# Down projection of a streaming-encoder layer: six of eleven channel pairs through seven block products, the rest plain, and the residual parked in DRAM

## The chip, the cores and the metric

The kernel runs on one core of a Trainium2 chip. A core has a matrix engine (TensorE, PE in the profile; its weight loads are PEld), a vector engine (VectorE, DVE), a scalar engine (ScalarE, ACT), GpSimd (POOL) and SyncE (SP), which here issues nearly all DMAs. Each runs its own instruction list in order; semaphores join them. The metric is the time of one execution on the device in microseconds (us); lower is better.

## The reference, cut to what matters

One layer: three token mixers, a cross-attention into a memory, and a gated MLP, all in float32, on 512 tokens of 1024 channels. The change is in the last step of the MLP:

```python
def conv_ffn(h, w_up, conv_w, conv_b, w_down):
    u = causal_dwconv(h @ w_up, conv_w) + conv_b      # 1024 -> 2 x 2816, then 3 taps over time
    a, b = jnp.split(u, 2, axis=-1)
    return (jax.nn.silu(a) * b) @ w_down              # 2816 -> 1024
...
x = x + conv_ffn(rmsnorm(x, norm_ffn[l]), w_up[l], ffn_conv[l], ffn_conv_b[l], w_down[l])
```

The hidden 2816 channels are 22 chunks of 128 (NF); the 1024 output channels are 8 blocks of 128 (KC). So `w_down` is 8 x 22 blocks of 128 x 128.

## The kernel before, in words

All activations lie with channels on the 128 partitions and the 512 tokens along the row. A float32 product is made of three passes: each operand is split into a rounded high part and the remainder, and PE adds hi x hi, hi x lo and lo x hi into one PSUM bank (`mm3`, lines 193 to 201). The high part is written by ACT (a copy with rounding), the low part by DVE (a subtraction).

**Weights** come in units of 128 x 1024 floats, which are eight 128 x 128 blocks. `split_unit` (171 to 178) loads one by SP's DMA queue into `wraw` (3 buffers), ACT writes `whi` (2 buffers) and DVE writes `wlo` (2 buffers). So a unit's split waits until PE has finished with the unit two before it.

**Up projection** (loop at 1098 to 1120): for each of the 22 chunks m it makes two 128 x 512 outputs, then `gated` (1068 to 1080) adds the convolution taps (`uc`, DVE) and multiplies the halves into `hid[m]`. Chunks in `SEVEN` go through `seven_products` (1027 to 1066): the product of a 2 x 2 matrix of weight blocks and a 2 x 2 matrix of input blocks (channel halves x token halves L and R of 256 tokens) is made with seven block products in place of eight. The sums of input blocks are formed once by `token_forms` (982 to 1003, at m = FORMS = 4), the sums of weight blocks for each m (1037 to 1043), and sums of products are taken apart by DVE afterwards (1060 to 1065). Each product is 128 x 128 weights by 256 columns.

**Splitting the hidden chunks**: `split_hidden` (1089 to 1096) splits `hid[k]` into `hh` (four chunks in one `hquad` or `nquad` tile) and `hidl`. `SPLITS` says after which m how many are split: 4 after 18, 14 after 19, 3 after 20, the last one after the loop. The four `hquad` tiles hold the token forms until the last of the seven products (m = 20) is done; the four `nquad` tiles hold the split input of the up projection until m = 21 is done.

**Down projection** (1124 to 1137): for each of the 8 output blocks, 22 chunks x 3 matmuls of 512 columns into one PSUM bank, then DVE adds the residual `x3[m]` and SP stores the block. The residual lies in SBUF all the while (two `xquad` tiles of 1 MB, in the pool `late`).

**Order**: the program is written without semaphores. A planner orders each engine's instructions by a simulation of its own from the order of the code, and allots buffers from pools: a tile of a pool with n buffers waits for the release of an earlier one. `tc.issue_after` only fixes an order on one engine. PSUM has eight banks: 3 of `dense_ps`, 3 of `misc_ps`, 2 of `gdn_ps` (111 to 118).

Of the kernel before, what the change touches and what calls it, by code (L numbers as in the profile page):

```python
# [21 lines left out]
UB = 8  # L22
SPARE = 2
RAW_UP = 4
FORMS = 4
NORMS = {0: 2, 1: 6}
SEVEN = (7, 8, 9, 11, 13, 15, 16, 17, 18, 20)
SPLITS = {18: 4, 19: 14, 20: 3}
WARM = 9
LOADS = (0, 1, 3, 2, 4, 5, 6, 7, 8, 9, 10)  # L30
KEYS_AFTER = (2, 3, 4, 5)
# [4 lines left out]
T = 512  # L36
KC = D // P
# [38 lines left out]
def build(nc, tc, ctx, x_t, mem_t, w, cols_d, const_d, unit_d, out_t, dbg=None):  # L76
# [25 lines left out]
    zquad = tiles_of("cross", "zq", 4, (4, T))  # L102
    hidden = tiles_of("hidden", "hid", NF + SPARE)
    nquad = tiles_of("hidden", "nx", 4, (4, T))
    uwork = tiles_of("hidden", "u", UB)
    wsum = tiles_of("hidden", "ws", 2, (1024,))
    wsumh = tiles_of("hidden", "wsh", 2, (1024,))
    wsuml = tiles_of("hidden", "wsl", 2, (1024,))
    ptile = tiles_of("pair", "p", FYP[2])

    def dense_ps(name):
        return pd.tile([P, T], F32, tag="d", name=name)
# [90 lines left out]
    def block(i, n=P):  # L203
        return slice(i * P, i * P + n)
# [82 lines left out]
    def open_pool(name, stack, **kw):  # L287
        pool[name] = stack.enter_context(tc.tile_pool(name=name, bufs=1, **kw))
# [518 lines left out]
        V.tensor_tensor(lo, mixed[m], hi.bitcast(F32), ALU.subtract)  # L807
        ms.append((hi, lo))
    mixing.close()
    open_pool("late", ctx, side="right")  # L810
    cross = ExitStack()
    open_pool("cross", cross)

    xr = []
    for i in range(2):
        t = xquad(f"xr{i}")
        nc.sync.dma_start(t, x_t[:, 4 * i:4 * i + 4])
        xr += [t[:, m] for m in range(4)]

    mem_sb = load_mem("mem_sb", ztile)  # L820
# [161 lines left out]
    def token_forms():  # L982


        pairs = []
        for name in ("14", "23"):
            pairs.append([hquad(f"t{name}{z}", F32R).rearrange("p a b -> p (a b)").rearrange("p (f k n) -> p f k n", f=2, k=4)
                          for z in "hl"])
        for k in range(4):
            e, o = values[k], values[k + 4]  # L990
            f = uwork(f"tf{k}")

            def two(t):
# [90 lines left out]
        mm3(ps, split_unit(UNITS["up"] + 2 * m + z), [block(k) for k in range(KC)], x, True, True)  # L1084
        return ps

    hs2 = []

    def split_hidden():
        k = len(hs2)  # L1090
        if k % 4 == 0:
            quad[:] = [(hquad if k < 16 else nquad)(f"hh{k}", F32R)]
        hi, lo = quad[0][:, k % 4], hidden(f"hidl{k}", F32R)
        S.activation(hi, hid[k], AF.Copy)
        V.tensor_tensor(lo, hid[k], hi.bitcast(F32), ALU.subtract)
        hs2.append((hi, lo))

    for m in range(NF):
        if m in SEVEN:
            us = seven_products(m)  # L1100
        else:
            us = []
            for z in range(2):
                with ExitStack() as behind:
                    for i in ([root_mm] if m == 0 and z else [root_mm, root_sq, root] if m == 1 else []):
                        behind.enter_context(tc.issue_after(i.ins))
                    us.append(up_product(m, z, xf if m < RAW_UP else xn))
            if m < RAW_UP:
                raw, us = us, []
                for z, ps in enumerate(raw):  # L1110
                    t = uwork(f"u{m + NF * z}")
                    V.tensor_tensor(t, ps, r_f, ALU.mult)
                    us.append(t)
        gated(m, us)
        for _ in range(NORMS.get(m, 0)):
            up_norm()
        if m == FORMS:
            t_forms = token_forms()
        for _ in range(SPLITS.get(m, 0)):
            split_hidden()  # L1120
    while len(hs2) < NF:
        split_hidden()

    unit = None
    for m in range(KC):
        ps = dense_ps(f"dn{m}")
        k = 0
        while k < NF:
            c = m * NF + k
            if c % 8 == 0:  # L1130
                unit = split_unit(UNITS["down"] + c // 8)
            n = min(8 - c % 8, NF - k)
            mm3(ps, unit, [block(c % 8 + i) for i in range(n)], hs2[k:k + n], k == 0, k + n == NF)
            k += n
        o = uwork(f"out{m}")
        V.tensor_tensor(o, ps, x3[m], ALU.add)
        nc.sync.dma_start(out_t[m], o)


def constants():  # L1140
# [21 lines left out]
def layout(inputs):  # L1162
    f = np.float32
    g = {k: np.asarray(v) for k, v in inputs.items()}

    def tiles(a, n):

        k, m = a.shape
        t = a.reshape(k // P, P, m // P, P).transpose(2, 0, 1, 3).reshape(-1, 8, P, P)
        t = t.transpose(0, 2, 1, 3).reshape(-1, P, 1024)  # L1170
        assert t.shape[0] == n, t.shape
        return t

    def tokens(a):

        return a.reshape(4, 2, P, 512).transpose(0, 2, 1, 3).reshape(4, P, 1024)

    def by_head(a):

        return tiles(a, 12).reshape(3, H, P, 1024).transpose(1, 0, 2, 3).reshape(12, P, 1024)  # L1180

    wi = g["w_in"][0]
    w = np.empty((NUNITS, P, 1024), f)

    def put(name, t):
# [12 lines left out]
    put("woa", tiles(g["w_oa"][0], 4))  # L1198
    put("wob", tiles(g["w_ob"][0], 4))
    put("woc", tiles(g["w_oc"][0], 4))  # L1200
    put("wout", tiles(g["w_out"][0], 8))
    put("mq", tiles(g["w_mq"][0], 4))
    put("mo", tiles(g["w_mo"][0], 4))
    up = tiles(g["w_up"][0], 44)
    put("up", up.reshape(2, NF, P, 1024).transpose(1, 0, 2, 3).reshape(44, P, 1024))
    put("down", tiles(g["w_down"][0], 22))
# [49 lines left out]
```

## Time and profile before

| | |
|---|---|
| Median of 3 runs | 1055.1 us (1054.78 to 1057.11) |
| Profiled execution, its own time | 1056.93 us |
| Its span, from first to last instruction | 1055.3 us |
| Granted TensorE clock | 1.0 of full speed in all 40 slices |
| PE, PEld, DVE, ACT busy | 99%, 82%, 67%, 52% of the span |
| DMA | 96.39 MB, mean 91 GB/s |

The up projection stands between 693 and 928.6 us, the down projection from 928.6 to the end. A line of a group gives line, engine, operation, output and input tiles, count, then busy time and mean duration; a line of the timeline gives start, duration and the same names, with the idle time before it in brackets. A duration contains the engine's pipeline, so successive instructions overlap: the step from one start to the next is the throughput. A line of a table by stretches gives the length, then busy us and count for PE, PEld, DVE, ACT and POOL, the granted clock, the DMA share and GB/s. A line of waits says who waited for whom: us in total, times, the longest.

### The profile page before, as it was taken

How to read it: one execution, taken by the hardware profiler on the slowest of the kernel's cores; microseconds unless marked ns; L12 is line 12 of the kernel's file. 1: busy time of each engine (PE TensorE's matmuls, PEld its weight loads, DVE VectorE, ACT ScalarE, POOL GpSimd, SP SyncE). 2: the span in 40 equal slices, each digit the busy share in tenths (PEclk: the TensorE clock that was granted, in tenths of full speed). 3: DMA queues.
4: the chain of work that ended last, by engine and by line, in shares of the span. 5: the costliest groups of instructions: out<-in, count | busy, mean ns of one | idle time of the engine just before them, and what ended most of it. 6: DMA issues, size and time to landing. Idle time of an engine off the chain costs nothing.

```text
span 1055.3 us, 13641 instructions
## 1 busy us (share of the span) xinstructions
PE 1041.4 (99%) x5205; PEld 866.2 (82%) x5205; DVE 711.8 (67%) x1161; ACT 552.5 (52%) x912; POOL 28.7 (3%) x82
## 2 busy tenths in 40 slices
PE   9999999999999999999999999999999999999998
PEld 7778888778887888888887887878899999988886
DVE  5787768788555443456667748679898899973221
ACT  6376758646243644655445757555555545741220
POOL 0000000101010000000000000000000000000000
PEclk9999999999999999999999999999999999999999
DMA  6322211212111111213523323122323232323330
GB/s 233 97 84 100 78 63 60 71 60 80 61 60 61 61 60 55 86 61 100 179 88 132 124 97 111 38 91 80 100 100 120 90 112 100 101 80 124 116 120 20
DMA packets 28001, 96.39 MB, mean 91 GB/s; under 512 B 3232, under 2 KB 3488, under 8 KB 27680
## 3 DMA queue, kind: packets, MB, share of 16 engines
q1 hardware_dynamic: 27648, 95.26, 26.9%
q8 instruction: 41, 0.67, 0.2%
q10 hardware_dynamic: 288, 0.27, 0.1%
q14 instruction: 24, 0.20, 0.1%
HBM read 93.41 MB, written 2.10 MB: 91 GB/s over the span
## 4 chain that ended last, share of the span: by engine, by line
PE 94%; DVE 2%; ACT 1%; issue 1%; DMA 1%; SPq 0%; POOL 0%; ACTq 0%; DVEq 0%; POOLq 0%
PE g L197 4%; PE up L200 4%; PE g L198 4%; PE up L198 4%; PE up L197 4%; PE dn L200 4%; PE dn L198 4%; PE dn L197 4%; PE g L200 4%; PE gk L368 2%; PE px L1019 2%; PE px L1017 2%; PE f L197 1%; PE s L198 1%; PE s L200 1%; PE f L200 1%
## 5 line engine op out<-in xcount | busy, mean ns | idle before, releaser
L176 ACT ACTIVATE whi<-wraw 128x1024 fp32r<-128x1024 f32 x143 | 151.5, 1060 | 234.2 <-PE dn L198 82.3
L177 DVE TENSOR_TENSOR wlo<-wraw,whi 128x1024 fp32r<-128x1024 f32 x143 | 174.5, 1220 | 98.2 <-PE dn L200 46.3
L197 PE MATMUL g<-hh,whi 128*128 128x512 f32 x192 | 77.5, 404 | 1.6 <-DVE gate L384 1.6
L198 PE MATMUL g<-hl,whi 128*128 128x512 f32 x192 | 75.8, 395 | 0.0
L198 PE MATMUL dn<-hidl,whi 128*128 128x512 f32 x176 | 69.3, 395 | 0.0
L197 PE MATMUL dn<-hh,whi 128*128 128x512 f32 x176 | 69.3, 394 | 0.0
L200 PE MATMUL g<-hh,wlo 128*128 128x512 f32 x192 | 51.5, 401 | 0.0
L197 PE MATMUL up<-xnh,whi 128*128 128x512 f32 x128 | 50.5, 394 | 0.0
L198 PE MATMUL up<-xnl,whi 128*128 128x512 f32 x128 | 50.5, 394 | 0.0
L200 PE MATMUL dn<-hh,wlo 128*128 128x512 f32 x176 | 45.4, 395 | 0.0
L197 PEld LDWEIGHTS g<-hh,whi 128*128 128x128 f32 x192 | 36.1, 188 | 10.8 <-DVE gate L384 1.4
L200 PEld LDWEIGHTS g<-hh,wlo 128*128 128x128 f32 x192 | 35.8, 188 | 8.3 <-issue 0.5
L198 PEld LDWEIGHTS g<-hl,whi 128*128 128x128 f32 x192 | 36.2, 188 | 7.7
L1075 DVE SCALAR_TENSOR_TENSOR uc<-u,cols,uc 128x511 f32<-128x511 f32 (+1 forms) x56 | 39.8, 749 | 0.0
L200 PEld LDWEIGHTS dn<-hh,wlo 128*128 128x128 f32 x176 | 33.2, 188 | 7.8
L198 PEld LDWEIGHTS dn<-hidl,whi 128*128 128x128 f32 x176 | 33.2, 188 | 7.7
L197 PEld LDWEIGHTS dn<-hh,whi 128*128 128x128 f32 x176 | 33.1, 188 | 7.7
L384 DVE TENSOR_TENSOR gate<-g,r_x 128x512 f32<-128x512 f32 x24 | 16.4, 688 | 30.8 <-PE g L200 30.8
L1023 ACT ACTIVATE whi<-wraw 128x1024 fp32r<-128x1024 f32 (+1 forms) x20 | 16.9, 846 | 31.6 <-PE px L1017 15.9
L200 PE MATMUL up<-xnh,wlo 128*128 128x512 f32 x128 | 32.4, 395 | 0.0
L197 PEld LDWEIGHTS up<-xnh,whi 128*128 128x128 f32 x128 | 24.1, 189 | 5.2
L198 PEld LDWEIGHTS up<-xnl,whi 128*128 128x128 f32 x128 | 24.1, 188 | 5.2
(924 smaller groups left out, 2757.7 us busy)
## 6 DMA issues: line engine op xcount, KB each, us to landing
wraw<-w SPq DMA_DIRECT2D x166, 512.0 KB, 3.4
x<-x_t SPq DMA_DIRECT2D x8, 256.0 KB, 6.6
xr<-x_t SPq DMA_DIRECT2D x2, 1024.0 KB, 6.3
out<-out SPq DMA_DIRECT2D x8, 256.0 KB, 2.0
mem_sb<-mem_t SPq DMA_DIRECT2D x4, 256.0 KB, 5.0
wraw<-w SPq DMA_DIRECT2D x2, 256.0 KB, 4.3
inv<-unit ACTq DMA_DIRECT2D x1, 256.0 KB, 3.5
const<-const SPq DMA_DIRECT2D x1, 194.0 KB, 6.0
```

Source lines behind the costliest of these rows:

```text
L176: S.activation(hi, raw, AF.Copy)
L177: V.tensor_tensor(lo, raw, hi.bitcast(F32), ALU.subtract)
L197: PE.matmul(ps, hi[:, b], xh, start=first and i == 0, stop=False)
L198: PE.matmul(ps, hi[:, b], xl, start=False, stop=False)
L200: mm = PE.matmul(ps, lo[:, b], xh, start=False, stop=last and i == len(xs) - 1)
L368: pin(PE.matmul(first[h], a[:, c:c + P], b, start=k == 0 and a is hi and b is xh, stop=k == KC - 1 and b is xl))
L384: V.tensor_tensor(dst, ps, r_x, ALU.mult)
L1017: PE.matmul(ps, wh[:, block(i)], xl[:, i], start=False, stop=False, skip_group_check=not new)
L1019: PE.matmul(ps, wl[:, block(i)], xh[:, i], start=False, stop=i == 3, skip_group_check=not new)
L1023: S.activation(hi, src, AF.Copy)
L1075: V.scalar_tensor_tensor(c[:, s:], u[:, :T - s], col("ffn_conv", 3 * j + 2 - s), c[:, s:], ALU.mult, ALU.add)
```

## The change

1. Of the 11 pairs of hidden chunks (2j, 2j + 1), those with j in `JS` = 5 to 10 go through seven block products; the ten chunks 0 to 9 stay plain. The 2 x 2 blocks are here: two output blocks x the two chunks of the pair, by the two chunks x two token halves.
2. `form_pair` makes and splits, for each of the six pairs, the blocks and sums of blocks of the hidden chunks, after the up loop. The slots for all split parts (`slot`) come from the `hquad` tiles, then the `nquad` tiles, then a new pool `extra` of 8 tiles, then `hidden`.
3. `seven_down` takes 12 of the 22 weight units; a unit holds the four blocks of two pairs. ACT and DVE split three of the four (768 columns) and split the sums of blocks (1024 columns), which DVE forms. Each of the 7 products is 2 pairs x 3 passes of 256 columns. Products that belong to one output half alone go straight into the banks of the plain part (`o0`, `o1`); those that several outputs share go to two further banks `px` and `pz`, which `rest` reads out.
4. The output blocks are worked in two groups of four banks. In the first all 40 plain blocks come first, then two output pairs of three units each; in the second 24 plain blocks come first, then the two pairs, and 16 plain blocks last (`PLAIN_AT`).
5. The residual is written to DRAM once (two 1 MB DMAs after m = 4), which frees the pool `late` for `extra`; `rest` reads it back, 256 KB for each output block.
6. In the up projection m = 17 leaves `SEVEN` and becomes plain, and `SPLITS` becomes 10 after m = 18 (the plain chunks).
7. The host lays the down weights out in the order in which they are used.

```diff
+JS = (5, 6, 7, 8, 9, 10)
+FORM_SLOTS = 8
+PLAIN_AT = 40, 24
...
-SEVEN = (7, 8, 9, 11, 13, 15, 16, 17, 18, 20)
-SPLITS = {18: 4, 19: 14, 20: 3}
+SEVEN = (7, 8, 9, 11, 13, 15, 16, 18, 20)
+SPLITS = {18: 10}
...
+    extra = tiles_of("extra", "e", FORM_SLOTS)
...
+    spilled = ctx.enter_context(tc.tile_pool(name="spill", bufs=1, space=bass.MemoryType.DRAM)).tile(
+        [P, KC, T], F32, tag="x3", name="x3_spill")
...
+    def slot(name):
+
+        if not slots:
+            n = len(slots_from)
+            if n < 8:
+                t = (hquad if n < 4 else nquad)(f"room{n}", F32R)
+                slots.extend(t[:, i] for i in range(4))
+            else:
+                slots.append(extra(f"room{n}", F32R) if n < 8 + FORM_SLOTS else hidden(f"room{n}", F32R))
+            slots_from.append(n)
+        return slots.pop(0)
+
+    slots_from = []
+    plain = [k for k in range(NF) if k // 2 not in JS]
+    hs2, forms = {}, {}
+
+    def split_into(src, hi, lo):
+        S.activation(hi, src, AF.Copy)
+        V.tensor_tensor(lo, src, hi.bitcast(F32), ALU.subtract)
+        return hi, lo
 
     def split_hidden():
...
+        k = plain[len(hs2)]
+        hs2[k] = split_into(hid[k], slot(f"hh{k}"), hidden(f"hidl{k}", F32R))
+
+    def form_pair(j):
+        e, o = hid[2 * j], hid[2 * j + 1]
+        left = slot(f"el{j}")
+        b11 = split_into(e[:, L], left[:, L], left[:, R])
+        b2 = split_into(o, slot(f"oh{j}"), slot(f"ol{j}"))
+        f = uwork(f"f{j}")
...
+        V.tensor_tensor(e[:, L], e[:, R], e[:, L], ALU.subtract)
+        V.tensor_tensor(two(f), two(e), o[:, None, R].to_broadcast([P, 2, T // 2]), ALU.add)
+        V.tensor_tensor(e[:, R], o[:, L], f[:, L], ALU.subtract)
+        t14 = split_into(e, slot(f"t14h{j}"), slot(f"t14l{j}"))
+        t23 = split_into(f, slot(f"t23h{j}"), slot(f"t23l{j}"))
...
+        forms[j] = {1: b11, 2: half(b2, L), 3: half(b2, R), 4: half(t14, R), 5: half(t14, L), 6: half(t23, L), 7: half(t23, R)}
...
         if m == FORMS:
             t_forms = token_forms()
+            for i in range(2):
+                nc.sync.dma_start(spilled[:, 4 * i:4 * i + 4], x_quads[i])
+            late.close()
+            open_pool("extra", ctx, side="right")
         for _ in range(SPLITS.get(m, 0)):
             split_hidden()
-    while len(hs2) < NF:
+    while len(hs2) < len(plain):
         split_hidden()
...
+    for j in JS:
+        form_pair(j)
+
+
+    opened = {}
+
+    def into(ps, lhs, rhs, z=slice(0, T), last=False):
+
+        first = opened.get(id(ps), (None, None))[1]
+        with ExitStack() as order:
+            if first is not None:
+                order.enter_context(tc.issue_after(first.ins))
+            mm = PE.matmul(ps[:, z], lhs, rhs, start=first is None, stop=last, skip_group_check=True)
+        opened.setdefault(id(ps), (ps, mm))
+
+    def plain_products(u, blocks):
+        for at in range(0, len(blocks), 8):
+            hi, lo = split_unit(u + at // 8)
+            part = blocks[at:at + 8]
+            for ps in {id(b): b for b, _ in part}.values():
+                mine = [(block(i), hs2[k]) for i, (b, k) in enumerate(part) if b is ps]
+                for b, (xh, xl) in mine:
+                    into(ps, hi[:, b], xh)
+                    into(ps, hi[:, b], xl)
+                for i, (b, (xh, _)) in enumerate(mine):
+                    into(ps, lo[:, b], xh, last=i == len(mine) - 1)
+        return u + len(blocks) // 8
+
+    def seven_down(u, o0, o1, px, pz):
+
+
+        for g in range(len(JS) // 2):
+            raw = load_unit(u + g)
+            a = raw.rearrange("p (f n) -> p f n", f=4)
+            hi, lo = (wp.tile([P, 1024], F32R, tag=t, name=f"{t}{u + g}", bufs=b) for t, b in (("whi", WB[1]), ("wlo", WB[2])))
+            split_into(raw[:, 256:], hi[:, :768], lo[:, :768])
+            st = wsum(f"sd{u + g}")
+            s4 = st.rearrange("p (f n) -> p f n", f=4)
+            V.tensor_tensor(s4[:, :2], a[:, 0:1].to_broadcast([P, 2, 256]), a[:, 1:3], ALU.subtract)
+            V.tensor_tensor(s4[:, 2], a[:, 1], s4[:, 1], ALU.subtract)
+            V.tensor_tensor(s4[:, 3], a[:, 3], s4[:, 2], ALU.subtract)
+            sh, sl = split_into(st, wsumh(f"sdh{u + g}", F32R), wsuml(f"sdl{u + g}", F32R))
+            for ps, z, n, (wh, wl), at in ((px, L, 1, (hi, lo), 0), (o1, L, 4, (hi, lo), 1), (o0, L, 2, (hi, lo), 2), (px, R, 5, (sh, sl), 1),
+                                           (pz, R, 7, (sh, sl), 0), (pz, L, 6, (sh, sl), 2), (o0, R, 3, (sh, sl), 3)):
+                for q in range(2):
+                    b = slice(256 * at + P * q, 256 * at + P * q + P)
+                    xh, xl = forms[JS[2 * g + q]][n]
+                    into(ps, wh[:, b], xh, z)
+                    into(ps, wh[:, b], xl, z)
+                    into(ps, wl[:, b], xh, z, last=q == 1 and g == len(JS) // 2 - 1)
+        return u + len(JS) // 2
+
+    def rest(m, px, pz):
+
+        v, w = uwork(f"v{m}d"), uwork(f"w{m}d")
+        S.activation(v, px, AF.Copy)
+        V.tensor_tensor(w[:, R], pz[:, L], v[:, L], ALU.add)
+        V.tensor_tensor(w[:, L], pz[:, R], w[:, R], ALU.add)
+        V.tensor_tensor(v[:, R], w[:, R], v[:, R], ALU.add)
+        V.tensor_tensor(w[:, R], pz[:, R], v[:, R], ALU.add)
+        for z, t in enumerate((v, w)):
+            x_in = uwork(f"x3_{m + z}")
+            nc.sync.dma_start(x_in, spilled[:, m + z])
+            V.tensor_tensor(t, t, x_in, ALU.add)
+        return v, w
+
+    def finish(m, banks, rests):
+        for z, (ps, t) in enumerate(zip(banks, rests)):
+            V.tensor_tensor(t, ps, t, ALU.add)
+            nc.sync.dma_start(out_t[m + z], t)
+
+    u = UNITS["down"]
+    for m in range(0, KC, 4):
+        banks = [dense_ps(f"dn{m}"), misc_ps(f"dn{m + 1}"), dense_ps(f"dn{m + 2}"), misc_ps(f"dn{m + 3}")]
+        blocks = [(b, k) for b in banks for k in plain]
+        at = PLAIN_AT[m // 4]
+        u = plain_products(u, blocks[:at])
+        for q in range(2):
+            px, pz = (dense_ps(f"dx{m}"), misc_ps(f"dz{m}")) if q == 0 else (gdn_ps(f"dx{m + 2}"), gdn_ps(f"dz{m + 2}"))
+            u = seven_down(u, banks[2 * q], banks[2 * q + 1], px, pz)
+            r = rest(m + 2 * q, px, pz)
+            if at < len(blocks) and q:
+                u = plain_products(u, blocks[at:])
+            finish(m + 2 * q, banks[2 * q:2 * q + 2], r)
```

More of the change, by code (lines that the diff above doesn't have):

```diff
@@ L809, in build @@
     mixing.close()
-    open_pool("late", ctx, side="right")
+    late = ExitStack()
+    open_pool("late", late, side="right")
     cross = ExitStack()
     open_pool("cross", cross)
-    xr = []
+    xr, x_quads = [], []
     for i in range(2):
@@ L817, in build @@
         nc.sync.dma_start(t, x_t[:, 4 * i:4 * i + 4])
+        x_quads.append(t)
         xr += [t[:, m] for m in range(4)]
@@ L1085, in up_product, with two, half @@
         return ps
-    hs2 = []
-    def split_hidden():
[L1090 to L1096, printed above, removed]
+    slots = []
+    def slot(name):
[15 more added lines that the diff above has]
+        return hi, lo
+    def split_hidden():
+        k = plain[len(hs2)]
[6 more added lines that the diff above has]
+        f = uwork(f"f{j}")
+        def two(t):
+            return t.rearrange("p (f n) -> p f n", f=2)
+        V.tensor_tensor(e[:, L], e[:, R], e[:, L], ALU.subtract)
[3 more added lines that the diff above has]
+        t23 = split_into(f, slot(f"t23h{j}"), slot(f"t23l{j}"))
+        def half(pair, z):
+            return tuple(t[:, z] for t in pair)
+        forms[j] = {1: b11, 2: half(b2, L), 3: half(b2, R), 4: half(t14, R), 5: half(t14, L), 6: half(t23, L), 7: half(t23, R)}
     for m in range(NF):
@@ L1118, in build @@
             t_forms = token_forms()
+            for i in range(2):
+                nc.sync.dma_start(spilled[:, 4 * i:4 * i + 4], x_quads[i])
+            late.close()
+            open_pool("extra", ctx, side="right")
         for _ in range(SPLITS.get(m, 0)):
             split_hidden()
-    while len(hs2) < NF:
+    while len(hs2) < len(plain):
         split_hidden()
[L1124 to L1137, printed above, removed]
+    for j in JS:
+        form_pair(j)
@@ L1205, in layout @@
     put("up", up.reshape(2, NF, P, 1024).transpose(1, 0, 2, 3).reshape(44, P, 1024))
-    put("down", tiles(g["w_down"][0], 22))
+    wd = g["w_down"][0].reshape(NF, P, 4, 2, P).transpose(2, 3, 0, 1, 4)
+    chunks = [k for k in range(NF) if k // 2 not in JS]
+    parts = []
+    for p, at in zip((0, 2), PLAIN_AT):
+        flat = [wd[q, z, k] for q in (p, p + 1) for z in range(2) for k in chunks]
+        parts += flat[:at]
+        for q in (p, p + 1):
+            for i in range(0, len(JS), 2):
+                parts += [wd[q, z, 2 * j + odd] for z, odd in ((1, 0), (0, 0), (1, 1), (0, 1)) for j in JS[i:i + 2]]
+        parts += flat[at:]
+    put("down", np.stack(parts).reshape(22, 8, P, P).transpose(0, 2, 1, 3).reshape(22, P, 1024))
     ws = np.zeros((P, KC, P), f)
```

## The prediction

> **What bounds the kernel now.** I read the page's busy shares first, then its chain of work.
>
> ```profile
> span 1055.3 us, 13641 instructions
> PE 1041.4 (99%) x5205; PEld 866.2 (82%) x5205; DVE 711.8 (67%) x1161; ACT 552.5 (52%) x912; POOL 28.7 (3%) x82
> PE 94%; DVE 2%; ACT 1%; issue 1%; DMA 1%; SPq 0%; POOL 0%; ACTq 0%; DVEq 0%; POOLq 0%
> ```
>
> PE is busy throughout and is 94% of the chain. So a change in matmul work counts in full, unless another engine then fails to feed PE. Next come the matmuls of the down projection (tile dn) and PE's waits from 690 us on.
>
> ```profile
> L197 PE MATMUL dn<-hh,whi x176: 390/392/404, 928.6 to 1049.0; 128*128 128x512 f32 x176
> L200 PE MATMUL dn<-hh,wlo x176: 390/393/404, 932.3 to 1051.1; 128*128 128x512 f32 x176
> PE up L198 <- DVE xfl L190: 0.7, 2, 0.5
> ```
>
> The duration of 392 ns overlaps the next matmul; what counts is the step from start to start. The 3 x 176 = 528 matmuls start between 928.6 and 1051.1: 122.5 / 527 = 0.2324 us each, 122.7 us in all, with no hole. PE's only wait in the last 365 us is 0.7 us near their beginning. Now the same step for 256 columns, from the timeline of the up projection's seven products:
>
> ```profile
> 819.95 0.28 PE L1013 MATMUL px<-xnh,whi 128*128 128x256 f32 x1
> ...
> 823.52 0.64 PE L1019 MATMUL px<-xnh,sl 128*128 128x256 f32 x4
> 824.00 0.39 PE L197 MATMUL up<-xnh,whi 128*128 128x512 f32 x1
> ```
>
> Between 819.95 and 824.00 lie 34 half-wide matmuls: 4.05 / 34 = 0.1191 us each. Two halves (0.2382) thus cost 0.0058 more than one full matmul; that tax is paid on each pair. Third, the engine busy times around the hand-over from up to down (length, PE, PEld, DVE, ACT):
>
> ```profile
> 870.00:890.00 20.00, 20.00 (x170) 20.00 (x169) 19.75 (x31) 12.91 (x18) 0.00 (x0) 1.00 0.26 82
> 890.00:910.00 20.00, 20.00 (x125) 17.90 (x124) 19.13 (x30) 12.09 (x16) 0.00 (x0) 1.00 0.29 103
> 910.00:929.00 19.00, 19.00 (x114) 16.85 (x114) 18.30 (x31) 16.85 (x29) 0.00 (x0) 1.00 0.30 95
> 929.00:943.00 14.00, 14.00 (x62) 11.33 (x61) 12.98 (x18) 6.07 (x9) 0.00 (x0) 1.00 0.33 113
> 943.00:1055.00 112.00, 108.47 (x467) 87.60 (x465) 28.10 (x27) 19.22 (x19) 0.00 (x0) 1.00 0.27 92
> ```
>
> DVE was 57.2 of 59 us busy (97%) before the down projection, 13.0 of 14 in it, and then only 28.1 of 112. PE waited in none of it. The change puts work into that empty 112 us.
>
> **PE, part by part.** Down before: 528 x 0.2324 = 122.7 us. After, the plain part is 10 chunks x 8 outputs x 3 = 240 full matmuls, 55.8 us; the seven products are 4 output pairs x 3 units x 7 products x 2 channel pairs x 3 = 504 halves, 60.0 us. Sum 115.8: minus 6.9 us. Six pairs by plain blocks would be 288 full ones, 66.9 us; the seventh eighths alone would save 8.4, and the tax (252 x 0.0058) takes 1.5 of it. In the up projection m = 17 leaves SEVEN: 48 full (11.2) for 84 halves (10.0), plus 1.2 us. Net on PE: -5.7 us.
>
> **DVE, the engine that must feed this.** Steps again from start to start:
>
> ```profile
> 902.47 0.42 DVE L1063 TENSOR_TENSOR u<-w,v 128x256 f32<-128x256 f32 x1
> 902.80 0.42 DVE L1064 SCALAR_TENSOR_TENSOR u<-py,w 128x256 f32<-128x256 f32 x1
> ...
> 904.07 1.22 DVE L1024 TENSOR_TENSOR sl<-s,sh 128x1024 fp32r<-128x1024 f32 x1
> 905.20 1.41 DVE L1075 SCALAR_TENSOR_TENSOR uc<-u,cols,uc 128x511 f32<-128x511 f32 x2
> 906.53 0.75 DVE L1075 SCALAR_TENSOR_TENSOR uc<-up,cols,uc 128x511 f32<-128x511 f32 x1
> ...
> 922.63 2.50 DVE L1095 TENSOR_TENSOR hidl<-hid,hh 128x512 fp32r<-128x512 f32 x4
> 925.03 0.43 DVE L1065 TENSOR_TENSOR u<-px,w 128x256 f32<-128x256 f32 x1
> ```
>
> 256 wide takes 0.33, 512 wide 2.40 / 4 = 0.60, 1024 wide 1.13, a uc step 0.66; 768 wide, which no row has, I put at 0.87, midway. Then:
> - A form_pair: splits of 256 and 3 x 512, sums of 256, 512, 256: 3 x 0.33 + 4 x 0.60 = 3.4 us, six times 20.4. Before, the twelve chunks cost 12 x 0.60 = 7.2, most of it inside the up projection.
> - A unit of the seven: 0.87 + 0.60 + 2 x 0.33 + 1.13 = 3.3 us against 42 x 0.1191 = 5.0 of PE.
> - rest and finish: 4 x 0.33 + 4 x 0.60 = 3.7 us for each output pair, so 3 x 3.3 + 3.7 = 13.6 of DVE in each 15.0 of PE (91%).
> - A plain unit: 1.13 against 24 x 0.2324 = 5.6.
> - m = 17 plain instead of seven: four sums of 512, splits of 3 x 1024 and 512, five steps of 256 (8.0 us) become two splits (2.3): DVE gains 5.7 us ahead of the hand-over.
>
> Total in the down projection: 20.4 + 39.6 + 11.3 + 14.8 + 3.2 (the last uc steps and hid) = 89 of 115.8 us. That fits, but bunched. Call t0 PE's first down matmul. The plain 40 blocks cover PE until t0 + 27.9; the three seven units start at 27.9, 32.9 and 37.9. DVE must have done by then, besides 3.2 of uc and hid and three plain splits (3.4): two forms and a unit by the first (16.7 us), four and two by the second (26.8), six and three by the third (36.9). The third is the tightest: 1.0 us of slack, or 4.4 if j = 5 is formed ahead of t0 (six of its seven slots come from hquad, free once m = 20's products are done; the nquad slots wait for m = 21). The nearest rows are the 97% windows without a PE wait. I allow 0.5 us of stall: 0 if DVE keeps that density, 1.1 if one 1024-wide split comes late. Below nothing is excluded, since PE had no wait to lose. ACT adds per unit about what DVE's two splits need, and has half its time free.
>
> **Moves that I cost at nothing.**
>
> ```profile
> wraw<-w SPq DMA_DIRECT2D x166, 512.0 KB, 3.4
> xr<-x_t SPq DMA_DIRECT2D x2, 1024.0 KB, 6.3
> SPq L1137 <- DVE out L1136: 39.6, 8, 15.0
> 1051.50 0.69 DVE L1136 TENSOR_TENSOR out<-dn,xr 128x512 f32<-128x512 f32 x1 [9.88 <-PE dn L200]
> 1052.22 0.34 SPq L1137 DMA_DIRECT2D out<-out  x1
> ```
>
> The two 1 MB stores of x at m = 4 are like the two 1 MB loads (6.3 us); two of them ahead of a weight load make it land at about 16 us at worst. Three raw and two split buffers hold some 2 to 3 units of 5.6 us, which covers it; with the cover gone it would be up to 5 us. The eight 256 KB reads and the out stores stand in SP's order before later weight loads; SP already sat 15.0 us on one out store without PE noticing. After the last matmul there is, as now, one add and one store; the 16 plain blocks kept for the end (11.2 us) hide the last rest (3.7). PSUM: the second half's first banks are freed by finish more than 10 us ahead.
>
> Sum: -5.7 + 0.5 = -5.2. The profiled execution took 1056.93 (span 1055.3 and 1.6 around it), 1.8 over the median of the runs, so it would be 1051.7 there; on the median 1055.1 it gives 1049.9.
>
> **Rival 1: DVE falls behind in the seven stretches.** At the 93% density of 929 to 943, the 36.9 us take 39.7: 1.8 late at the third unit. And where output pair follows pair (twice), px completes at the moment that the split buffers of the unit after next come free; if DVE does rest and finish (3.7) before that unit's splits (0.87 + 1.13), it takes 5.75 of 5.0: 0.75 late, twice. Together 3.3: 1052.6, or 1051.5 to 1054.5 with one part less or more. For it: 91% load. Against: 97% went without a wait.
>
> **Rival 2, slower: the forms stand before the weight splits.** In the code all forms precede the down units. DVE is in order; if the forms of j = 6 to 10 (17.0) after the 3.2 of uc stand before the third plain unit's wlo (1.13), it comes at t0 + 21.3 (24.7 with j = 5 also late). PE needs it at 16 x 3 x 0.2324 + 8 x 0.2324 = 13.0. PE waits 8.3 to 11.7: net +2.6 to +6.0, 1057.7 to 1061.1. It decides once over 8 us of forms stand ahead. What the order does now:
>
> ```profile
> 916.92 6.36 ACT L1094 ACTIVATE hh<-hid 128x512 fp32r<-128x512 f32 x12
> 927.10 2.50 DVE L1095 TENSOR_TENSOR hidl<-hid,hh 128x512 fp32r<-128x512 f32 x4
> 929.50 1.23 DVE L177 TENSOR_TENSOR wlo<-wraw,whi 128x1024 fp32r<-128x1024 f32 x1
> 930.64 1.42 DVE L1075 SCALAR_TENSOR_TENSOR uc<-u,cols,uc 128x511 f32<-128x511 f32 x2
> 931.96 0.70 DVE L1095 TENSOR_TENSOR hidl<-hid,hh 128x512 fp32r<-128x512 f32 x1
> ```
>
> For it: twelve hh in one run on ACT. Against: a down unit's wlo went in at 929.50 between hidl steps that the code puts before it.
>
> **Rival 3: weight loads set the pace.** The change adds loads: 744 for 528 in down, 48 for 84 in up, 180 more.
>
> ```profile
> 819.83 0.19 PEld L1013 LDWEIGHTS px<-xnh,whi 128*128 128x128 f32 x1
> 819.95 0.19 PEld L1017 LDWEIGHTS px<-xnl,whi 128*128 128x128 f32 x1
> ```
>
> If each 0.19 us load stood in front of its matmul, that would be 180 x 0.19 = 34.2 us, net +28.5: 1083.6. But loads start 0.12 apart while the matmul before them streams, so they hide. The Trainium skill ("TensorE: Matmul & The Clock Gate", section "The mechanism") says that a weight load overlaps a running matmul only if it goes to other rows of the array, which speaks against this change; these full-height loads overlap, so the trace disagrees. By that page's load of 128 / 1.2 = 107 ns (section "LDWEIGHTS (loading the stationary operand)") the 180 would cost 19 us, an estimate.
>
> **How the numbers follow.** Forecast 0.62 (1048.4 to 1051.5: from no stall to a whole late split, and 1.0 on either side, somewhat under half of the 2.3 between the runs), rival 1 0.21, rival 2 0.15, rival 3 0.01, anything else 0.01. No change means within 0.2%, 2.1 us, about what can be told here: 1053.0 to 1057.2. Faster: 0.62 and half of rival 1, 0.72. Same: the other half and a little of rival 2, 0.13. Slower: 0.15. Forecast and rival 1 together hold 0.83, so the range is 1048.4 to 1055.0; the forecast's own is 1048.4 to 1051.5.
>
> **What would show it.** Right: 240 full and 504 half matmuls from first to last in 116 to 117 us, steps of 0.232 and 0.119, DVE near 90% in the seven stretches, PE's waits under 1 us. Rival 1: PE waits on wlo or sl at the third unit and after px. Rival 2: one wait of 8 us or more on wlo about 13 us into down, with split_into lines before it on DVE. The forecast is wrong if half matmuls step at more than 0.125 with three products per block in turn (504 x 0.006 = 3 us), or if PE waits over 2 us.

## The result, and the profile after

The changed kernel takes 1049.34 us (median of 4 runs, 1048.82 to 1050.53), the kernel before 1054.94 us in the same set (median of 4). The ratio is 0.9944 with a 95% interval of 0.9927 to 0.9962: 5.6 us or 0.6% faster. Timed again on another occasion beside other kernels (a0 below) it was 0.9949 [0.9935, 0.9962]. The prediction said 1049.9 us. The profiled execution took 1050.53 us, where the prediction had 1051.7 for it.

The page of the changed kernel: span, busy shares, chain by engine.

```profile
span 1048.8 us, 14151 instructions
PE 1035.8 (99%) x5385; PEld 871.1 (83%) x5385; DVE 756.6 (72%) x1252; ACT 566.8 (54%) x936; POOL 28.7 (3%) x82
PE 94%; DVE 2%; ACT 1%; issue 1%; DMA 1%; SPq 0%; POOL 0%; ACTq 0%; DVEq 0%; POOLq 0%
```

PE is 5.6 us less busy with 180 more matmuls (5385 for 5205), DVE 44.8 us more. PE is still 99% of the span, so the gain is PE's. Next the matmuls of the tile dn (first and last start), and all that PE waited for from 690 us on.

```profile
L1186 PE MATMUL dn<-room,whi x176: 277/285/404, 929.1 to 1042.5; 128*128 128x256 f32 x96, 128*128 128x512 f32 x80
L1186 PE MATMUL dn<-room,wlo x128: 274/392/404, 932.8 to 1044.6; 128*128 128x512 f32 x80, 128*128 128x256 f32 x48
PE up L204 <- DVE xfl L196: 0.7, 2, 0.5
```

The down projection runs from 929.1 to 1044.6 plus one step: 115.7 us, 122.7 before. In it PE waits for nothing; the 0.7 us are those that were there before. The step of the 256-wide matmuls comes from two lines of the timeline that stand one unit apart:

```profile
956.99 0.39 PE L1186 MATMUL dx<-room,whi 128*128 128x256 f32 x2
...
962.00 0.39 PE L1186 MATMUL dx<-room,whi 128*128 128x256 f32 x2
```

One unit is 42 half matmuls, 5.01 / 42 = 0.1193 us each; the up projection's had 0.1191. Three products per weight block in turn, high and low parts alternating, cost no more than the older order. The busy times by stretches of the down projection (length, PE, PEld, DVE, ACT):

```profile
929.00:943.00 14.00, 14.00 (x62) 11.36 (x61) 14.00 (x23) 7.92 (x13) 0.00 (x0) 1.00 0.23 76
943.00:957.00 14.00, 14.00 (x62) 11.32 (x62) 12.24 (x22) 7.57 (x11) 0.00 (x0) 1.00 0.34 112
957.00:972.00 15.00, 15.00 (x128) 15.00 (x127) 13.82 (x25) 6.54 (x9) 0.00 (x0) 1.00 0.35 107
972.00:988.00 16.00, 16.00 (x133) 15.82 (x132) 12.12 (x20) 6.99 (x9) 0.00 (x0) 1.00 0.48 155
988.00:1003.00 15.00, 15.00 (x66) 12.18 (x65) 13.35 (x24) 4.03 (x4) 0.00 (x0) 1.00 0.56 187
1003.00:1018.00 15.00, 15.00 (x124) 14.83 (x123) 9.90 (x14) 6.10 (x7) 0.00 (x0) 1.00 0.41 138
1018.00:1033.00 15.00, 15.00 (x129) 15.00 (x128) 9.92 (x15) 5.57 (x6) 0.00 (x0) 1.00 0.33 109
1033.00:1049.00 16.00, 11.99 (x56) 9.53 (x54) 4.49 (x9) 0.00 (x0) 0.00 (x0) 0.97 0.08 33
```

PE is full in every stretch up to its last matmul, at 1044.6 us. The counts of about 128 in 15 us mark the seven products, those of 62 to 66 the plain blocks. DVE is full only in the first 14 us; to 988 us it is busy for 52.2 of 59 us.

The spans differ by 6.5 us, of which 0.7 have nothing to do with the edit: the up projection's first matmul came at 693.1 us in the trace of before and at 692.4 in this one.

```profile
L197 PE MATMUL up<-xfh,whi x64: 390/393/404, 693.1 to 737.0; 128*128 128x512 f32 x64
```

```profile
L203 PE MATMUL up<-xfh,whi x64: 390/393/404, 692.4 to 736.3; 128*128 128x512 f32 x64
```

From there to the first down matmul it is 235.5 us before (928.6 - 693.1) and 236.7 after (929.1 - 692.4): m = 17 costs 1.2 us. The down projection is 7.0 us shorter, and the tail is the same: from the last matmul's start to the end of the span 4.2 us both times. Sum: -0.7 + 1.2 - 7.0 = -6.5.

### The profile page after: what moved, and what is told of

It reads as the page before. It is cut to its first block, busy times and chain, and to the rows that moved or that the text cites. A ratio compares the mean times of both kernels' runs of the same rounds, so it can differ in the third digit from the quotient of the medians.

```text
span 1048.8 us, 14151 instructions
## 1 busy us (share of the span) xinstructions
PE 1035.8 (99%) x5385; PEld 871.1 (83%) x5385; DVE 756.6 (72%) x1252; ACT 566.8 (54%) x936; POOL 28.7 (3%) x82
## 4 chain that ended last, share of the span: by engine, by line
PE 94%; DVE 2%; ACT 1%; issue 1%; DMA 1%; SPq 0%; POOL 0%; ACTq 0%; DVEq 0%; POOLq 0%
PE dn L1186 8%; PE up L206 5%; PE up L204 4%; PE up L203 4%; PE g L203 4%; PE g L204 4%; PE g L206 4%; PE gk L374 2%; PE px L1027 2%; PE px L1025 2%; PE dz L1186 2%; PE dx L1186 2%; PE f L203 1%; PE s L206 1%; PE s L204 1%; PE f L206 1%
## 5 line engine op out<-in xcount | busy, mean ns | idle before, releaser
L182 ACT ACTIVATE whi<-wraw 128x1024 fp32r<-128x1024 f32 x133 | 140.7, 1058 | 169.3 <-PE g L204 38.7
L183 DVE TENSOR_TENSOR wlo<-wraw,whi 128x1024 fp32r<-128x1024 f32 x133 | 162.1, 1219 | 44.4 <-ACT whi L182 19.6
L204 PE MATMUL up<-xnl,whi 128*128 128x512 f32 x144 | 56.8, 394 | 0.0
L203 PE MATMUL up<-xnh,whi 128*128 128x512 f32 x144 | 56.8, 394 | 0.0
L1186 PE MATMUL dn<-room,whi 128*128 128x256 f32 (+1 forms) x176 | 49.6, 333 | 0.0
L203 PEld LDWEIGHTS g<-hh,whi 128*128 128x128 f32 x192 | 36.1, 188 | 10.9 <-DVE gate L390 1.4
L1186 PE MATMUL dn<-room,wlo 128*128 128x512 f32 (+1 forms) x128 | 34.1, 352 | 0.0
L1186 PEld LDWEIGHTS dn<-room,whi 128*128 128x128 f32 x176 | 29.8, 188 | 3.4
L206 PEld LDWEIGHTS up<-xnh,wlo 128*128 128x128 f32 x144 | 27.0, 188 | 6.2
L1186 PE MATMUL dn<-hidl,whi 128*128 128x512 f32 x80 | 31.6, 395 | 0.0
L1186 PEld LDWEIGHTS dn<-room,wlo 128*128 128x128 f32 x128 | 24.0, 188 | 3.5
```

The source lines that it names most:

```text
L182: S.activation(hi, raw, AF.Copy)
L183: V.tensor_tensor(lo, raw, hi.bitcast(F32), ALU.subtract)
L203: PE.matmul(ps, hi[:, b], xh, start=first and i == 0, stop=False)
L204: PE.matmul(ps, hi[:, b], xl, start=False, stop=False)
L206: mm = PE.matmul(ps, lo[:, b], xh, start=False, stop=last and i == len(xs) - 1)
L1186: mm = PE.matmul(ps[:, z], lhs, rhs, start=first is None, stop=last, skip_group_check=True)
```

## The experiments

Twelve runs, each timed beside the kernel before on the same chip. a0, e1, e2 and e6 were timed together; where another run is set against a0 below, the medians come from different occasions or chips, on which the kernel before differs by up to 0.3 us. "Against before" is the difference of the medians; the ratio has its 95% interval. A wait counts from the end of the matmul before it. A 256-wide matmul lasts 0.28 us and steps by 0.119, so from start to start PE loses 0.16 us more for each wait than the table says.

| Run | Median | Before | Against before | Ratio | PE waits in the down projection |
|---|---|---|---|---|---|
| a0 changed kernel again | 1050.29 | 1054.88 | -4.6 | 0.9949 [0.9935, 0.9962] | none |
| e1 m = 17 seven again | 1050.38 | 1054.88 | -4.5 | 0.9956 [0.9944, 0.9969] | 1.3 us |
| e2 four pairs | 1052.20 | 1054.88 | -2.7 | 0.9974 [0.9964, 0.9984] | none |
| e6 m = 17 plain alone | 1055.88 | 1054.88 | +1.0 | 1.0008 [0.9999, 1.0017] | none |
| e5 parking alone | 1055.26 | 1055.05 | +0.2 | 1.0003 [0.9994, 1.0013] | none |
| e4 cover of 24 blocks | 1051.96 | 1055.05 | -3.1 | 0.9968 [0.9956, 0.9981] | 1.6 us |
| e7 forms first | 1062.13 | 1055.05 | +7.1 | 1.0065 [1.0051, 1.0079] | 10.9 us, one |
| e8 more work per form | 1055.43 | 1055.05 | +0.4 | 1.0003 [0.9994, 1.0013] | 3.4 us |
| e11 sums on GpSimd | 1055.28 | 1055.16 | +0.1 | 1.0001 [0.9992, 1.0010] | 3.7 us |
| e9 m = 17 and sums on GpSimd | 1052.95 | 1055.16 | -2.2 | 0.9976 [0.9967, 0.9986] | 2.3 us |
| e10 four more sevens, sums on GpSimd | 1077.73 | 1055.16 | +22.6 | 1.0208 [1.0194, 1.0222] | 4.6 us, and 17.2 in the up projection |
| e12 units in order | 1049.44 | 1055.04 | -5.6 | 0.9951 [0.9937, 0.9964] | none |

The theory to be tested was the prediction's: PE's work alone sets the time, and DVE has just enough room. The rivals: DVE falls behind in the seven stretches (1), the forms stand before the weight splits (2).

**a0, the changed kernel again.** No edit.

> The changed kernel itself, unedited, timed beside the three kernels of this set so that they have a partner on the same chip. Theory (PE sets the time; 6.9 us less matmul work in the down projection, 1.2 more in the up projection, everything else hidden): 5.2 to 5.8 us under the kernel before. A rival that rests on chance in the four runs so far: under 4 us.

4.6 us by the medians, 5.4 by the ratio of 0.9949. The four runs were no accident, and single sets differ by about a microsecond.

**e2, four pairs.**

```diff
-JS = (5, 6, 7, 8, 9, 10)
+JS = (7, 8, 9, 10)
...
-PLAIN_AT = 40, 24
+PLAIN_AT = 56, 40
...
-SPLITS = {18: 10}
+SPLITS = {18: 14}
```

> The changed kernel with four pairs (j = 7 to 10) through the seven products and fourteen plain chunks. Theory: each pair is worth 6.9 / 6 = 1.15 us of PE, so 2.3 us slower than the changed kernel, with 336 full and 336 half matmuls, all in 118.1 us. Rival (part of the gain is lost to DVE in the bunched stretches): less than 1.5 us slower, since DVE has 6.8 us of forms less to make.

Tile dn of this kernel, first and last start:

```profile
L1186 PE MATMUL dn<-room,whi x176: 279/392/404, 927.9 to 1043.8; 128*128 128x512 f32 x112, 128*128 128x256 f32 x64
L1186 PE MATMUL dn<-room,wlo x144: 278/392/404, 931.6 to 1045.9; 128*128 128x512 f32 x112, 128*128 128x256 f32 x32
```

927.9 to 1045.9 plus a step is 118.2 us, against the 118.1 of the sum and 115.7 with six pairs. The median is 1.9 us over a0. So a pair is worth what its matmuls say, 1.15 us, and 6.8 us less of DVE work gave nothing back: DVE cost the changed kernel no time.

**e6, m = 17 plain alone** (on the kernel before).

```diff
-SEVEN = (7, 8, 9, 11, 13, 15, 16, 17, 18, 20)
+SEVEN = (7, 8, 9, 11, 13, 15, 16, 18, 20)
```

> The kernel before with only m = 17 taken out of the seven products. Theory: 1.2 us slower than the kernel before (48 full matmuls for 84 halves), since PE did not wait there. Rival (DVE at 97% costs PE time that the trace does not show): the same or faster.

Its tiles up (first start) and dn (first start):

```profile
L197 PE MATMUL up<-xfh,whi x64: 390/392/404, 692.4 to 736.4; 128*128 128x512 f32 x64
```

```profile
L197 PE MATMUL dn<-hh,whi x176: 390/393/404, 929.2 to 1049.5; 128*128 128x512 f32 x176
```

The up projection takes 236.8 us, 1.3 more than before; the median is 1.0 us higher, though the interval of the ratio just reaches 1. The trace shows the term, the time alone would not quite.

**e1, m = 17 back among the seven products** (on the changed kernel): the same edit the other way round.

> The changed kernel with m = 17 put back among the seven products of the up projection. Theory: PE has 1.2 us less work (84 halves x 0.1191 for 48 x 0.2324), DVE 5.7 us more ahead of the hand-over. If PE alone sets the time: 1.2 us faster than the changed kernel, no PE wait. Rival (DVE needs the relief at the hand-over): PE waits for wlo, sl or a form within 40 us after the first down matmul, and the time is the same or up to 5 us longer.

Nothing is gained that these medians can show: 1050.38 against 1050.29. PE's waits:

```profile
PE dn L1186 <- ACT whi L1116: 0.8, 1, 0.8
PE up L204 <- DVE xfl L196: 0.7, 2, 0.5
PE dx L1186 <- ACT sdh L1116: 0.4, 1, 0.4
```

Two new waits of 1.3 us together, both near 970 us (1.6 from start to start), use up the 1.2 us that m = 17 saves on PE. ACT is named, so the lines of the timeline around them, of DVE, ACT and PE:

```profile
967.12 0.42 DVE L1214 TENSOR_TENSOR sd<-wraw,sd 128x256 f32<-128x256 f32 x1
...
969.00 0.84 ACT L1116 ACTIVATE whi<-wraw 128x768 fp32r<-128x768 f32 x1 [3.91 <-PE dn L1186]
969.75 1.04 ACT L1116 ACTIVATE sdh<-sd 128x1024 fp32r<-128x1024 f32 x1
...
969.90 0.50 PE L1186 MATMUL dn<-room,whi 128*128 128x256 f32 x2 [0.82 <-ACT whi L1116]
...
970.84 0.51 PE L1186 MATMUL dx<-room,sdh 128*128 128x256 f32 x2 [0.45 <-ACT sdh L1116]
```

ACT stood idle for 3.91 us before its weight split, until PE's own matmuls set it free, and PE then waited for that split. The trace and the instruction list of the built program (each engine's instructions in the order that the planner chose) point to the buffer: there are two for the high parts (the second figure of `WB = (3, 2, 2)`), and in PE's list the third unit holds one of them until the sixth, because only 6 of its 42 matmuls come before the fourth unit's. The fourth, fifth and sixth unit share the other, so the fifth's split starts only when PE has made the fourth's high products. The split of the fourth unit's sums, ready from 967.54 (967.12 + 0.42), stood behind it on ACT and gave the second wait. Neither wait here is for DVE, as rival 1 would have it. No run had a third buffer, though, so that it would bring back the 1.2 us is not shown; nor is it that the third unit was held back because its forms come late from DVE.

**e8, more work per form.** The 512-wide sum of `form_pair` is written four times, each with the same result.

```diff
-        V.tensor_tensor(two(f), two(e), o[:, None, R].to_broadcast([P, 2, T // 2]), ALU.add)
+        for _ in range(4):
+            V.tensor_tensor(two(f), two(e), o[:, None, R].to_broadcast([P, 2, T // 2]), ALU.add)
```

> The changed kernel with the 512-wide sum of each form made four times in place of once, each time the same result: 18 more steps of 0.60 us, 10.9 us more DVE work at the hand-over. DVE was idle for some 6.8 us between 929 and 988 us in the changed kernel. If DVE was near its limit there: PE waits 4 us or more. If the planner can shift PE work into the gaps: under 2 us slower.

```profile
PE dz L1187 <- ACT room L1116: 1.5, 1, 1.5
PE dz L1187 <- DVE room L1117: 1.4, 1, 1.4
PE dn L1187 <- DVE room L1117: 0.5, 1, 0.5
```

This is DVE falling behind, as in rival 1, but on forms (room), where the rival had named wlo and sl. All three waits lie between 964 and 970 us; two are for a low part from DVE, the first for a high part from ACT. The kernel is 5.1 us over a0 by the medians, yet the waits sum to 3.4 (4.0 from start to start). Much of the rest is in the granted clock (the third figure from the end) of the stretches there:

```profile
965.00:970.00 5.00, 1.94 (x10) 1.54 (x11) 5.00 (x12) 3.04 (x6) 0.00 (x0) 0.95 0.01 2
970.00:975.00 5.00, 5.00 (x33) 5.00 (x33) 4.62 (x9) 2.11 (x3) 0.00 (x0) 0.71 0.10 18
```

After 3 idle us of 5, TensorE got 0.71 of its clock in the next 5 us and made 33 matmuls where 42 fit: 9 x 0.119 = 1.1 us more. In fact it had half its clock from 969.5 to 972.9 us, and there a half-wide matmul stepped by 0.213 us in place of 0.119. So 10.9 us of added DVE work cost about 5 us. Part of the rest went into DVE's idle time: from 929 to 978 us it was idle for 4.9 us in the changed kernel and for 1.6 here.

**e7, forms first.** What rival 2 feared, forced: the third plain unit's split is queued behind the last step of the last form.

```diff
+        last_form[:] = [V.tensor_tensor(t23l, f, t23h.bitcast(F32), ALU.subtract)]
...
-            hi, lo = split_unit(u + at // 8)
+            with ExitStack() as behind:
+                if u + at // 8 == UNITS["down"] + 2:
+                    behind.enter_context(tc.issue_after(last_form[0].ins))
+                hi, lo = split_unit(u + at // 8)
```

> The changed kernel with the split of the third plain down unit queued on DVE behind the last step of the last form, which is the order that the second rival feared. By its sum: DVE reaches the split at 21.3 to 24.7 us, PE needs it at 13.0; one PE wait of 8.3 to 11.7 us about 13 us into the down projection, 8 to 12 us slower than the changed kernel. Other theory (PE finds other work to do, or DVE makes up for it later): under 4 us.

The wait, the matmuls behind it in the timeline, and the clock:

```profile
PE dn L1191 <- DVE wlo L183: 10.9, 1, 10.9
```

```profile
955.86 3.63 PE L1191 MATMUL dn<-room,wlo 128*128 128x512 f32 x8 [10.89 <-DVE wlo L183]
```

```profile
950.00:955.00 5.00, 0.00 (x0) 0.00 (x0) 4.17 (x9) 1.34 (x3) 0.00 (x0) 0.50 0.00 0
955.00:960.00 5.00, 4.14 (x11) 3.32 (x12) 2.59 (x3) 1.06 (x1) 0.00 (x0) 0.58 0.59 179
```

One wait of 10.9 us, inside the 8.3 to 11.7 of the prediction; it begins 16 us after the first down matmul (929.0), because PE did all sixteen of that unit's high products and four of the next unit before it needed the low part (48 + 16 + 4 = 68 steps x 0.2324 = 15.8 us), where the prediction had counted eight and 13.0 us. The split came later too: the wait ended 26.9 us after the first down matmul (955.86 - 929.0), where the prediction had 21.3 to 24.7. So both ends of the wait lay 2 to 3 us later than in the sum, and that their difference fits is partly luck. The first eight matmuls after it take 3.63 us in place of 2.02, at half the clock; the 0.58 is a mean over 5 us in which the full clock came back at 959.2. The kernel is 11.8 us over a0 by the medians. The rival's price was about right; its condition is what the changed kernel does not meet.

**e4, cover of 24 blocks.**

```diff
-PLAIN_AT = 40, 24
+PLAIN_AT = 24, 24
```

> The changed kernel with 24 instead of 40 plain blocks ahead of the first seven products; the other 16 come in the code after the second output pair. The cover for the forms shrinks from 27.9 to 16.7 us. If the order of the code held on PE: the third unit would be due at 26.8 us with up to 36.9 us of DVE work, PE waits 6 to 10 us, 6 to 10 us slower than the changed kernel. Theory as the trace of the changed kernel suggests it (the planner takes units of the second output pair, or late plain blocks, where forms are late): no wait or under 2 us.

```profile
PE dn L1186 <- DVE room L1117: 0.9, 2, 0.4
PE dx L1186 <- DVE wlo L1117: 0.7, 1, 0.7
```

With 11.2 us less cover PE waits 1.6 us, not 6 to 10, and the median is 1.7 us over a0. PE's instruction list suggests why so little: PE does not run the units in the order of the code. Of the third unit's 42 matmuls 6 come before the fourth unit, which then runs whole, and the other 36 are strewn through the fifth, the sixth and the plain unit after it. So the third unit's last forms were not due where the prediction had them due. How much of the 11.2 us this saved, no run tells apart.

**e12, units in order.** Each unit's matmuls are queued behind the one that the code puts last in the unit before it, for the six units of the first half.

```diff
+            for g in gate:
+                order.enter_context(tc.issue_after(g.ins))
...
+            gate[:] = ends[-1:] if len(ends) < 6 else []
...
+            ends.append(newest[0])
```

> The changed kernel with PE held to the order of the code for the six seven-product units of the first half: no matmul of a unit before the last one of the unit before it. In the changed kernel the planner let PE mix units of the two output pairs, and the last forms were ready 49 us after the first down matmul, 11 us behind the moment at which the prediction had the third unit due. The prediction's sum (36.9 us of DVE work by 37.9, or 4.4 us of slack with one form made early): no wait over 1 us, 1050.3 again. Other theory (the mixing is what hides DVE's lateness): PE waits at the third unit, 2 to 11 us slower than the changed kernel.

1049.44 us and no wait. But the edit did less than it says. By PE's instruction list, in the changed kernel only 6 of the third unit's 42 matmuls come before the fourth unit's first, and the rest are strewn through the fourth, fifth and sixth. With the edit 27 come first, then the whole fourth unit, and the other 15 inside the fifth: the matmul that the code puts last can itself be issued early, and the edge holds only to that one. In e7 PE's list has all six units in strict code order, and no wait follows the one of 10.9 us; but there every form was made before the first of these units. Strict order with the forms still to be made was not tried, so whether PE would then wait stays open.

**e5, parking alone** (on the kernel before): the two stores after m = 4, `late` closed, and the eight reads.

```diff
...
+            for i in range(2):
+                nc.sync.dma_start(spilled[:, 4 * i:4 * i + 4], x_quads[i])
+            late.close()
...
-        V.tensor_tensor(o, ps, x3[m], ALU.add)
+        x_in = uwork(f"x3_{m}")
+        nc.sync.dma_start(x_in, spilled[:, m])
+        V.tensor_tensor(o, ps, x_in, ALU.add)
```

> The kernel before with only the residual parked in DRAM: two 1 MB stores after m = 4 and eight 256 KB reads in the down projection, which keeps its plain products. Theory: hidden, within 0.5 us of the kernel before, no PE wait. Rival (the stores delay weight loads, or the reads hold up SP or DVE): 2 to 5 us slower, PE waits near 745 us or in the down projection.

0.2 us, inside the interval; the traffic of 4 MB is hidden.

**e11, e9, e10: weight sums on GpSimd.** If DVE's room is the next limit, as e8 has it, then its sums could go to GpSimd, which is idle.

```diff
-            V.tensor_tensor(s4[:, :2], a[:, 0:1].to_broadcast([P, 2, 256]), a[:, 1:3], ALU.subtract)
-            V.tensor_tensor(s4[:, 2], a[:, 1], s4[:, 1], ALU.subtract)
-            V.tensor_tensor(s4[:, 3], a[:, 3], s4[:, 2], ALU.subtract)
+            G.tensor_tensor(s4[:, :2], a[:, 0:1].to_broadcast([P, 2, 256]), a[:, 1:3], ALU.subtract)
+            G.tensor_tensor(s4[:, 2], a[:, 1], s4[:, 1], ALU.subtract)
+            G.tensor_tensor(s4[:, 3], a[:, 3], s4[:, 2], ALU.subtract)
```

That is e11. e9 also puts m = 17 back into `SEVEN`; e10 further moves the four sums of `seven_products` and adds m = 10, 12 and 14.

> The changed kernel with the three sums of weight blocks of each of the 12 seven-product units on GpSimd in place of VectorE. VectorE has 12 x 1.27 = 15 us less work in the down projection. Theory: PE did not wait in the changed kernel, so the time stays (within 0.5 us of 1050.3) if GpSimd makes a unit's sums in under 5 us. Rival (GpSimd is too slow for the chain raw, sums, rounding, remainder, or slows VectorE's own steps): PE waits on sdh or sdl, 2 us slower or more.

> As the kernel before this one, and m = 17 back among the seven products. With m = 17 alone put back, PE waited 1.3 us near 970 us and nothing was gained. Theory (that wait is VectorE's missing room at the hand-over): with 15 us less on VectorE the wait goes and the 1.2 us show: 1049.1. Rival (the wait comes from the order that the planner chose, or from ScalarE): 1050.3 again.

> The sums of weight blocks on GpSimd in the up projection too, and m = 10, 12, 14 and 17 added to the seven products. PE has 4 x 1.2 = 4.6 us less work; VectorE has per seven-product chunk 2.4 us less, and 4 x 3.3 us more for the added ones. Theory (VectorE's room is the only limit): 4.6 us faster than the changed kernel, 1045.7. Rival (thirteen seven-product chunks without plain ones between them meet another limit: PSUM banks, ScalarE, GpSimd's pace): PE waits in the up projection, less than 2 us gained or slower.

The theory misses in all three: e11 is 5.0 us over a0 by the medians, e9 2.7, e10 27. The groups of DVE's 768-wide split in the down projection, in a0 and then in e11:

```profile
L1117 DVE TENSOR_TENSOR wlo<-wraw,whi 128x768 fp32r<-128x768 f32 x12 | 11.5, 956 | 3.9 <-ACT whi L1116 3.3 <-PE dn L1186 0.6
```

```profile
L1117 DVE TENSOR_TENSOR wlo<-wraw,whi 128x768 fp32r<-128x768 f32 x12 | 17.3, 1443 | 7.0 <-PE dn L1186 4.7 <-ACT whi L1116 2.4
```

The same step takes 1443 ns in place of 956. Two lines of e11's timeline show why:

```profile
963.65 1.71 POOL L1212 TENSOR_TENSOR sd<-wraw 128x512 f32<-128x512 f32 x1 [6.59 <-DMA wraw<-w]
...
964.12 1.79 DVE L1117 TENSOR_TENSOR room<-f,room 128x512 fp32r<-128x512 f32 x1
```

GpSimd's sum takes 1.71 us where DVE's took 0.69, and it ends at 965.36. DVE's step of 0.69 us began at 964.12 and ended at 965.91: it stood still until GpSimd was done. Of the twelve 768-wide splits of e11, the eight that overlap a GpSimd sum took 1.40 to 2.02 us, the other four 0.95. A step that reads one input from PSUM was not held up:

```profile
993.46 1.46 POOL L1212 TENSOR_TENSOR sd<-wraw 128x512 f32<-128x512 f32 x1 [12.93 <-DMA wraw<-w]
...
994.25 0.42 DVE L1231 TENSOR_TENSOR w2d<-dz,w2d 128x256 f32<-128x256 f32 x1
```

The Trainium skill ("SBUF — State Buffer", section "SBUF: two separate sides") says that GpSimd and a DVE operation with two SBUF inputs share a pair of ports that one of them holds for its whole instruction; these rows agree. So much of the 15 us that were taken from DVE came back as standstill: from 957 to 972 us it was busy for 14.27 us, and with the sums, in the changed kernel, 13.82. PE's longest wait in e11 is 3.2 us, for a form's high part, and the half clock after it, from 973.0 to 979.8 us, adds to it. (The profiled execution is e11's slowest, at 1058.06 us, so its waits may be longer than usual.) e9 recovers some of e11's loss and stays 2.7 us slower than a0; e10's four added chunks make PE wait in the up projection too:

```profile
PE py L1027 <- DVE sl L1032: 5.0, 5, 1.8
PE px L1027 <- DVE wlo L1032: 4.2, 5, 1.4
```

No version here beats the changed kernel beyond the intervals; e12 comes to the same time.

## Why the prediction was right, point by point

- **PE, down: -6.9 predicted, -7.0 measured.** The counts are those of the sum, the steps 0.2324 and 0.1193. Shown by the trace, and by e2 (118.2 us against a sum of 118.1).
- **PE, up: +1.2 predicted, +1.2 measured** in the changed kernel; alone (e6) 1.3 in the trace.
- **DVE's work: 89 us predicted in the down projection, 89.8 measured** (the stretches from 929 to 1049). The estimate of 0.87 for the 768-wide step is good: one takes 0.96 us, and the 512 and 1024 wide ones, too, last 0.09 us longer than their step.
- **DVE hides: 0.5 us of stall allowed, 0 measured.** The result was right, but the working behind it was not, and that part of the right answer is luck. The prediction had the third unit due 37.9 us after the first down matmul, with 1.0 to 4.4 us of slack and all six forms done. In fact the last forms came at

```profile
977.80 0.68 DVE L1117 TENSOR_TENSOR room<-hid,room 128x512 fp32r<-128x512 f32 x1
978.41 0.68 DVE L1117 TENSOR_TENSOR room<-f,room 128x512 fp32r<-128x512 f32 x1
```

  which is 50 us after it. DVE had also been given the fourth and fifth unit and the sums of the sixth by then, and had stood idle for 4.9 us, each time waiting for ACT. PE did not notice since the rest of the third unit was placed among the fourth, fifth and sixth. So the slack that was worked out along the code's order is not the slack there was. What there was, e1 and e8 bound: with 5.7 us more work ahead of the hand-over PE waited for no step of DVE, with 10.9 us more in the forms it waited for three parts of forms, two of them DVE's.
- **DVE near 90% in the seven stretches:** 92% in the first (13.82 of 15), then 76%, and 66% in the second half (9.90 and 9.92 of 15). Late there too: rest and finish of a pair fell into the plain stretch that follows (13.35 of 15).
- **Parking at nothing:** right, shown by e5.
- **Rival 1** at 0.21 did not come; e8 shows that it can. (Its 5.75 us of DVE work in 5.0 is 5.7 by its own terms, 3.7 + 0.87 + 1.13, which changes nothing.) What e1 met first, by the trace the split buffer that the third unit holds, was in no rival. **Rival 2** at 0.15: its price was about right, with both ends of the wait 2 to 3 us late (e7), its condition not met. In the changed kernel the weight splits stand among the forms, as the rows of before had suggested. **Rival 3:** PEld is at 14.83 to 15.00 of 15 in the stretches of the seven products and PE still steps by 0.119.

## What to carry to other kernels

Where PE has no wait, price a change of its work by the step from start to start, shape by shape; here the terms of that kind came to -5.7 us, and -5.8 were measured. The engine that feeds PE must be added up for the stretch, not the kernel, and the sum by deadlines in code order is only a guide, because a planner may move PE's work as well. The next limit may be neither engine: here one more saving of 1.2 us was lost to waits that seem to come from a split buffer, which a unit held while it waited for its turn. That came out only when ACT's idle time was followed back to PE.

## What the runs showed of the hardware that was not expected

- **A long wait costs more than its length.** After 10.9 us without work TensorE ran at 0.50 of its clock for another 3.3 us (e7: 3.63 us for 2.02 us of matmuls). In e8 three waits of 1.5, 1.4 and 0.5 us, close together, were followed by 0.50 for 3.4 us, in e11 one of 3.2 us brought 0.50 for 6.8 us, which began within the wait. The Trainium skill ("TensorE: Matmul & The Clock Gate", section "What's actually happening") has the clock halve after a window of about 3.4 us of idleness; e7 agrees, and e8 and e11 show that no single wait need be that long. The waits of 0.4 to 0.8 us in e1 and e4 left the clock at 1.00.
- **An idle GpSimd is no free help to DVE:** 1.71 us for a sum of 0.69, and DVE's steps with two SBUF inputs stood still meanwhile (e11: 1.40 to 2.02 us for a split of 0.95), while those that read one input from PSUM did not (0.42 us as before).
- **The start of the up projection** came between 691.0 and 693.1 us in the traces of kernels that do not differ ahead of it. Differences of spans of that size need to be taken from a stage's own first matmul.
